# Matmul and layer norm on one core: the row-tile transposes move from TensorE to VectorE, and the start and the end of the kernel are rewritten

## The chip, the cores and the metric

The kernel runs on one core of a Trainium2 chip. The metric is device time in microseconds (us), the median over several executions. The profile of one execution has a span, from its first to its last instruction, which is about 2 us shorter than the timed value. In the profile PE is TensorE (PEld its weight loads), DVE is VectorE, ACT is ScalarE, POOL is GpSimd and SP is SyncE. L107 means line 107 of that kernel's file.

A ratio quoted below is the mean time of one kernel's fast runs over that of the fast runs of the kernel before in the same rounds, so it is not quite the ratio of the medians.

## The reference

```python
def setup_inputs():            # m = k = n = 2048, all float32
    return {"a": (2048, 2048), "b": (2048, 2048), "gamma": (2048,), "beta": (2048,), "eps": 1e-5}   # shapes, shortened

def reference(a, b, gamma, beta, eps):
    x = np.matmul(a, b)
    mean = np.mean(x, axis=-1, keepdims=True)
    var = np.var(x, axis=-1, keepdims=True)
    return gamma * (x - mean) / np.sqrt(var + eps) + beta
```

## The kernel before

The product is cut into 16 row tiles of 128 rows and 4 quarters of 512 columns. One (tile, quarter) needs 16 matmuls, one for each contraction tile of 128, and fills one PSUM tile of 128x512 fp32, called a bank here: 1024 matmuls in all. The program holds eight banks: seven for the product and one for transposes in this kernel, eight for both in the changed one. Each matmul needs the piece of `a` transposed. Both inputs are cast to fp16 while they are loaded.

Transposing is done on TensorE, for every tile, eight pieces into the one transpose bank, which ACT then copies out:

```python
    def emit_transposes_half(i, h):
        a16 = a16_lst[i]
        at = at_lst[i]
        t_ps = psum.tile([P, n_kt // 2, P], FP16, tag="tps", bufs=1, ...)
        for j in range(n_kt // 2):
            nc.tensor.transpose(t_ps[:, j, :], a16[:, ts(h * 8 + j, P)], ident)
        nc.scalar.copy(at[:, ds(h * 8, 8), :], t_ps)
```

The start takes the first four row tiles together with the left half of `b` (two quarters), so that each row of `b` that lands feeds eight matmuls. The loads bring tile 0, a row of `b`, tile 1, and so on, then the rest of `b`:

```python
    a16_lst[0] = emit_a_load(0, split=4)
    nc.gpsimd.dma_start(b16[:, 0, 0:NH], b[ts(0, P), 0:NH])
    ...
    a16_lst[1] = emit_a_load(1, split=2)
    nc.gpsimd.dma_start(b16[:, 1, 0:NH], b[ts(1, P), 0:NH])
    ...
    for kt in range(3, n_kt):
        nc.gpsimd.dma_start(b16[:, kt, 0:NH], b[ts(kt, P), 0:NH])
```

The scheduler of the framework chooses the order of instructions on each engine. In the steady part a tile's matmuls run over contraction tiles outside and quarters inside; the transposes of tile i+2 stand among them. Then each quarter gets its statistics (DVE) and is copied to SBUF (ACT), and DVE normalises from the copy with two operations per quarter:

```python
            for kt in range(n_kt):
                for q in range(n_nb):
                    emit_mm(i, q, kt)
                if kt == 4 and i + 2 < n_mt:
                    alloc_at(i + 2)
                    emit_transposes_half(i + 2, 0)
                if kt == 9 and i + 2 < n_mt:
                    emit_transposes_half(i + 2, 1)
            for q in range(n_nb):
                quarter_done(i, q)          # bn_stats on DVE, copy to SBUF on ACT
        emit_ln_stats(i)
        ...
        emit_ln_stt(i, ...)                 # 2 scalar_tensor_tensor per quarter on DVE, then the output DMA
```

Of the kernel before, what the change touches and what calls it, by code (L numbers as in the profile page):

```python
# [9 lines left out]
FP32 = mybir.dt.float32  # L10
FP16 = mybir.dt.float16
AluOp = mybir.AluOpType
# [4 lines left out]
def kernel(  # L17
# [9 lines left out]
    nc = tc.nc  # L27
    P = 128
    M, K = a.shape
    K2, N = b.shape  # L30
    assert K == K2
    assert M % P == 0 and K % P == 0 and N % 2048 == 0
    n_mt = M // P
    n_kt = K // P
    NB = 512
    n_nb = N // NB
    NH = N // 2

    n_start = 4
    assert n_mt > n_start  # L40

    if isinstance(eps, bass.AP):
        eps_ap = eps
        eps_val = None
    else:
        eps_ap = None
        eps_val = float(eps)

    konst = ctx.enter_context(tc.tile_pool(name="konst", bufs=1))
    bpool = ctx.enter_context(tc.tile_pool(name="bpool", bufs=1))  # L50
    a16p = ctx.enter_context(tc.tile_pool(name="a16p", bufs=4))
    atp = ctx.enter_context(tc.tile_pool(name="atp", bufs=6))
    xpool = ctx.enter_context(tc.tile_pool(name="xpool", bufs=20))
    upool = ctx.enter_context(tc.tile_pool(name="upool", bufs=4))
    cpool = ctx.enter_context(tc.tile_pool(name="cpool", bufs=2))
    stat = ctx.enter_context(tc.tile_pool(name="stat", bufs=4))
    psum = ctx.enter_context(tc.tile_pool(name="psum", bufs=1, space=bass.MemoryType.PSUM))

    gamma_b = konst.tile([P, N], FP32)
    beta_b = konst.tile([P, N], FP32)  # L60
    eps_t = konst.tile([P, 1], FP32)
    ident = konst.tile([P, P], FP16)

    b16 = bpool.tile([P, n_kt, N], FP16)

    def emit_a_load(i, split=1):
        a16 = a16p.tile([P, K], FP16, tag="a16", name=f"a16_{i}")
        w = K // split
        for s in range(split):
            nc.gpsimd.dma_start(a16[:, ds(s * w, w)], a[ts(i, P), ds(s * w, w)])  # L70
        return a16

    a16_lst = [None] * (n_mt + 2)
    at_lst = [None] * (n_mt + 1)

    def alloc_at(i):
        at_lst[i] = atp.tile([P, n_kt, P], FP16, tag="at", name=f"at{i}")

    def emit_transposes_half(i, h):
        a16 = a16_lst[i]  # L80
        at = at_lst[i]
        t_ps = psum.tile([P, n_kt // 2, P], FP16, tag="tps", bufs=1,
                         name=f"tps{i}_{h}")
        for j in range(n_kt // 2):
            nc.tensor.transpose(t_ps[:, j, :], a16[:, ts(h * 8 + j, P)], ident)  # L85
        nc.scalar.copy(at[:, ds(h * 8, 8), :], t_ps)  # L86

    def emit_transposes(i):
        alloc_at(i)
        emit_transposes_half(i, 0)  # L90
        emit_transposes_half(i, 1)
        return at_lst[i]

    bnst_l = [None] * n_mt
    c_ps_l = [[None] * n_nb for _ in range(n_mt)]
    x_sb_l = [[None] * n_nb for _ in range(n_mt)]
    rstd_l = [None] * n_mt
    mv_l = [None] * n_mt

    def alloc_q(i, q):  # L100
        if bnst_l[i] is None:
            bnst_l[i] = stat.tile([P, n_nb, 6], FP32, tag="bnst", name=f"bnst{i}")
        c_ps_l[i][q] = psum.tile([P, NB], FP32, tag="c_ps", bufs=7,
                                 name=f"cps_{i}_{q}")

    def emit_mm(i, q, kt):
        nc.tensor.matmul(  # L107
            c_ps_l[i][q],
            at_lst[i][:, kt, :],
            b16[:, kt, ds(q * NB, NB)],  # L110
            start=(kt == 0),
            stop=(kt == n_kt - 1),
        )

    def quarter_done(i, q):
        nc.vector.bn_stats(bnst_l[i][:, q, :], c_ps_l[i][q])  # L116
        x_sb = xpool.tile([P, NB], FP32, tag="x_sb", name=f"x_{i}_{q}")
        nc.scalar.copy(x_sb, c_ps_l[i][q])  # L118
        x_sb_l[i][q] = x_sb

    def emit_ln_stats(i):
        mv = stat.tile([P, 2], FP32, name=f"mv{i}")
        nc.vector.bn_aggr(mv, bnst_l[i])  # L123
        ve = stat.tile([P, 1], FP32, name=f"ve{i}")
        nc.vector.tensor_tensor(ve, mv[:, 1:2], eps_t, AluOp.add)  # L125
        sq = stat.tile([P, 1], FP32, name=f"sq{i}")
        nc.scalar.activation(sq, ve, ActFn.Sqrt)  # L127
        rstd = stat.tile([P, 1], FP32, name=f"rstd{i}")
        nc.vector.reciprocal(rstd, sq)  # L129
        mv_l[i] = mv  # L130
        rstd_l[i] = rstd

    def emit_ln_stt(i, split_out=2):
        mv, rstd = mv_l[i], rstd_l[i]
        c_sb = cpool.tile([P, N], FP32, tag="c_sb", name=f"c{i}")
        nq_per_out = n_nb // split_out
        for q in range(n_nb):
            qs = ds(q * NB, NB)
            u = upool.tile([P, NB], FP32, tag="u", name=f"u_{i}_{q}")
            nc.vector.scalar_tensor_tensor(  # L140
                u, x_sb_l[i][q], mv[:, 0:1], gamma_b[:, qs],
                AluOp.subtract, AluOp.mult,
            )
            nc.vector.scalar_tensor_tensor(  # L144
                c_sb[:, qs], u, rstd, beta_b[:, qs],
                AluOp.mult, AluOp.add,
            )
            if (q + 1) % nq_per_out == 0:
                o = ds((q + 1 - nq_per_out) * NB, nq_per_out * NB)
                nc.sync.dma_start(out[ts(i, P), o], c_sb[:, o])  # L150

    a16_lst[0] = emit_a_load(0, split=4)
    nc.gpsimd.dma_start(b16[:, 0, 0:NH], b[ts(0, P), 0:NH])
    nc.vector.memset(ident, 0.0)
    nc.gpsimd.affine_select(
        out=ident, in_=ident, compare_op=AluOp.not_equal, fill=1.0,
        base=0, pattern=[[-1, P]], channel_multiplier=1,
    )
    if eps_ap is not None:
        nc.sync.dma_start(eps_t, eps_ap.unsqueeze(0).to_broadcast([P, 1]))  # L160
    else:
        nc.vector.memset(eps_t, eps_val)
    a16_lst[1] = emit_a_load(1, split=2)
    nc.gpsimd.dma_start(b16[:, 1, 0:NH], b[ts(1, P), 0:NH])  # L164
    a16_lst[2] = emit_a_load(2, split=2)
    nc.gpsimd.dma_start(b16[:, 2, 0:NH], b[ts(2, P), 0:NH])  # L166
    a16_lst[3] = emit_a_load(3, split=2)
    for kt in range(3, n_kt):
        nc.gpsimd.dma_start(b16[:, kt, 0:NH], b[ts(kt, P), 0:NH])  # L169
    a16_lst[4] = emit_a_load(4)  # L170
    a16_lst[5] = emit_a_load(5)
    for kt in range(n_kt):
        nc.gpsimd.dma_start(b16[:, kt, NH:N], b[ts(kt, P), NH:N])  # L173
    nc.gpsimd.dma_start(gamma_b, gamma.unsqueeze(0).to_broadcast([P, N]))  # L174
    nc.gpsimd.dma_start(beta_b, beta.unsqueeze(0).to_broadcast([P, N]))  # L175
    for i in range(6, n_mt):
        a16_lst[i] = emit_a_load(i)

    startup_pairs_L = [(p, q) for p in range(n_start) for q in (0, 1)]
    startup_pairs_R = [(p, q) for p in range(n_start) for q in (2, 3)]  # L180
    for (p, q) in startup_pairs_L:
        alloc_q(p, q)
    for i in range(n_start):
        alloc_at(i)
    emit_transposes_half(0, 0)
    emit_transposes_half(0, 1)
    for q in (0, 1):
        emit_mm(0, q, 0)
    for p in range(1, n_start):
        emit_transposes_half(p, 0)  # L190
        emit_transposes_half(p, 1)
        for pp in range(p):
            for q in (0, 1):
                emit_mm(pp, q, p)
        for kt in range(p + 1):
            for q in (0, 1):
                emit_mm(p, q, kt)
    for kt in range(n_start, n_kt):
        for (p, q) in startup_pairs_L:
            emit_mm(p, q, kt)  # L200
    for (p, q) in startup_pairs_L:
        quarter_done(p, q)
    for (p, q) in startup_pairs_R:
        alloc_q(p, q)
    for kt in range(n_kt):
        for (p, q) in startup_pairs_R:
            emit_mm(p, q, kt)
        if kt == 0:
            at_lst[4] = emit_transposes(4)
        if kt == 2:  # L210
            at_lst[5] = emit_transposes(5)
    for (p, q) in startup_pairs_R:
        quarter_done(p, q)
    for p in range(n_start):
        emit_ln_stats(p)

    for i in range(n_start, n_mt):
        last = i == n_mt - 1
        for q in range(n_nb):
            alloc_q(i, q)  # L220
        if last:
            for q in range(n_nb):
                for kt in range(n_kt):
                    emit_mm(i, q, kt)
                quarter_done(i, q)
        else:
            for kt in range(n_kt):
                for q in range(n_nb):
                    emit_mm(i, q, kt)
                if kt == 4 and i + 2 < n_mt:  # L230
                    alloc_at(i + 2)
                    emit_transposes_half(i + 2, 0)
                if kt == 9 and i + 2 < n_mt:
                    emit_transposes_half(i + 2, 1)
            for q in range(n_nb):
                quarter_done(i, q)
        emit_ln_stats(i)
        if i - n_start < n_start:
            emit_ln_stt(i - n_start)
        emit_ln_stt(i, split_out=(2 if not last else 4))  # L240


# [32 lines left out]
```

## Time and profile before

| | |
|---|---|
| time | 268.0 us median of 15 (267.13 to 268.71) |
| span of the profiled execution | 265.8 us |
| TensorE busy | 242.6 us, of which product matmuls 230.0 |
| start of the last statistics (TensorE is done) | 255.16 us |
| DVE / ACT busy | 131.9 / 74.1 us |

Lines of the page of the kernel before: busy time by engine, then the chain of work that ended last (shares of the span), then groups of instructions (line, engine, operation, output from input, shapes, count, then busy us, mean ns of one, and idle time before with what ended it).

```profile
PE 242.6 (91%) x1280; PEld 116.6 (44%) x1280; DVE 131.9 (50%) x242; ACT 74.1 (28%) x114; POOL 30.2 (11%) x61
...
PE 89%; DMA 6%; DVE 2%; issue 1%; POOL 0%; DVEq 0%; POOLq 0%
PE cps L107 84%; PE tps L85 5%; DMA b<-in_b_dram 4%; DMA a<-in_a_dram 2%; DVE u L140 1%; DVE c L144 1%; POOL a L70 0%; DVE bnst L116 0%; DVEq L270 0%; DVE mv L123 0%; DVE ve L125 0%; DVE rstd L129 0%; POOLq L256 0%
...
L107 PE MATMUL cps<-b,at 128*128 128x512 f16 x1024 | 230.0, 381 | 5.6 <-DMA b<-in_b_dram 5.6
...
L85 PE MATMUL tps<-ident,a 128*128 128x128 f16 x256 | 22.3, 231 | 6.9 <-DMA a<-in_a_dram 6.8
```

The chain is 89% PE: whatever is taken from TensorE in the steady part comes off the time, as long as TensorE stays the chain there. The mean of 381 ns of one matmul overlaps with its neighbours (they are 0.2167 us apart, as the next lines show), so it is no cost. The cost is read from the chain in order of time (start us, length us, what), here the end of the start and then a stretch of the steady part:

```profile
8.22 9.45 DMA b<-in_b_dram
17.67 0.04 issue
17.71 1.01 PE cps L107 x2
18.72 0.85 PE tps L85 x8
19.57 2.13 PE cps L107 x5
...
88.62 0.45 PE tps L85 x8
89.07 9.55 PE cps L107 x44
98.62 0.45 PE tps L85 x8
99.07 4.32 PE cps L107 x20
103.38 0.45 PE tps L85 x8
```

In the steady part 64 matmuls take 9.55 + 4.32 = 13.87 us, 0.2167 us each, and 16 transposes take 0.90 us, 0.056 us each.

### The profile page before, as it was taken

How to read it: one execution, taken by the hardware profiler on the slowest of the kernel's cores; microseconds unless marked ns; L12 is line 12 of the kernel's file. 1: busy time of each engine (PE TensorE's matmuls, PEld its weight loads, DVE VectorE, ACT ScalarE, POOL GpSimd, SP SyncE). 2: the span in 40 equal slices, each digit the busy share in tenths (PEclk: the TensorE clock that was granted, in tenths of full speed). 3: DMA queues.
4: the chain of work that ended last, by engine and by line, in shares of the span. 5: the costliest groups of instructions: out<-in, count | busy, mean ns of one | idle time of the engine just before them, and what ended most of it. 6: DMA issues, size and time to landing. Idle time of an engine off the chain costs nothing.

```text
span 265.8 us, 3149 instructions
## 1 busy us (share of the span) xinstructions
PE 242.6 (91%) x1280; PEld 116.6 (44%) x1280; DVE 131.9 (50%) x242; ACT 74.1 (28%) x114; POOL 30.2 (11%) x61
## 2 busy tenths in 40 slices
PE   1369999999999999999999999999999999999930
PEld 1135444454444444454444444454544444444410
DVE  0000002400079089898989092745739091837753
ACT  1325101640064142323224151333133151303110
POOL 8443333440000000000000000000000000000000
PEclk9999999999999999999999999999999999999985
DMA  5999999999931615939375605230302112030304
GB/s 69 183 210 209 210 214 208 208 213 368 215 69 72 146 22 167 226 161 196 152 154 211 156 13 181 50 158 0 147 13 80 79 47 113 0 158 2 158 0 158
DMA packets 12974, 35.85 MB, mean 135 GB/s; under 512 B 1440, under 2 KB 1952, under 8 KB 12704
## 3 DMA queue, kind: packets, MB, share of 16 engines
q0 software_dynamic: 8064, 18.88, 37.7%
q1 hardware_dynamic: 4896, 16.78, 15.8%
q8 instruction: 10, 0.16, 0.3%
q14 instruction: 4, 0.03, 0.0%
HBM read 35.65 MB, written 16.78 MB: 197 GB/s over the span
## 4 chain that ended last, share of the span: by engine, by line
PE 89%; DMA 6%; DVE 2%; issue 1%; POOL 0%; DVEq 0%; POOLq 0%
PE cps L107 84%; PE tps L85 5%; DMA b<-in_b_dram 4%; DMA a<-in_a_dram 2%; DVE u L140 1%; DVE c L144 1%; POOL a L70 0%; DVE bnst L116 0%; DVEq L270 0%; DVE mv L123 0%; DVE ve L125 0%; DVE rstd L129 0%; POOLq L256 0%
## 5 line engine op out<-in xcount | busy, mean ns | idle before, releaser
L107 PE MATMUL cps<-b,at 128*128 128x512 f16 x1024 | 230.0, 381 | 5.6 <-DMA b<-in_b_dram 5.6
L107 PEld LDWEIGHTS <-at 128*128 128x128 f16 x1024 | 99.4, 98 | 121.0 <-issue 9.6
L116 DVE BATCH_NORM_STATS2 bnst<-cps 128x6 f32<-128x512 f32 x64 | 40.0, 685 | 127.8 <-PE cps L107 127.8
L118 ACT COPY x<-cps 128x512 f32<-128x512 f32 x64 | 37.3, 585 | 100.0 <-DVE bnst L116 99.1
L86 ACT COPY at<-tps 128x1024 f16<-128x1024 f16 x32 | 32.4, 1012 | 81.3 <-PE tps L85 81.3
L140 DVE SCALAR_TENSOR_TENSOR u<-x,mv,gamma_b 128x512 f32<-128x512 f32 x64 | 45.9, 743 | 0.0
L144 DVE SCALAR_TENSOR_TENSOR c<-u,rstd,beta_b 128x512 f32<-128x512 f32 x64 | 45.1, 745 | 0.0
L85 PE MATMUL tps<-ident,a 128*128 128x128 f16 x256 | 22.3, 231 | 6.9 <-DMA a<-in_a_dram 6.8
L85 PEld LDWEIGHTS <-a 128*128 128x128 f16 x256 | 18.6, 104 | 17.1 <-DMA a<-in_a_dram 7.6
L70 POOL DMA_DIRECT2D a<-in_a_dram x22 | 11.9, 548 | 106.1 <-PE tps L85 99.6
L173 POOL DMA_DIRECT2D b<-in_b_dram x16 | 8.4, 527 | 14.9 <-DMA b<-in_b_dram 11.0
L169 POOL DMA_DIRECT2D b<-in_b_dram x13 | 6.9, 527 | 9.7 <-DMA b<-in_b_dram 5.1
L123 DVE BATCH_NORM_AGGREGATE mv<-bnst 128x2 f32<-128x24 f32 x16 | 3.9, 254 | 0.4
L127 ACT ACTIVATE sq<-ve 128x1 f32<-128x1 f32 x16 | 3.1, 203 | 0.6 <-DVE ve L125 0.6
L125 DVE TENSOR_TENSOR ve<-mv,eps_t 128x1 f32<-128x1 f32 x16 | 2.3, 155 | 0.4
L129 DVE RECIPROCAL rstd<-sq 128x1 f32<-128x1 f32 x16 | 2.4, 157 | 0.3 <-ACT sq L127 0.3
L86 ACT ACT_TABLE_LOAD x1 | 1.3, 1283 | 0.7 <-PEq L256 0.7
L127 ACT ACT_TABLE_LOAD x1 | 1.3, 1283 | 0.0
L166 POOL DMA_DIRECT2D b<-in_b_dram x1 | 0.5, 532 | 1.2 <-DMA a<-in_a_dram 1.2
L175 POOL DMA_DIRECT2D beta_b<-in_beta_dram x1 | 0.5, 527 | 0.7 <-DMA b<-in_b_dram 0.7
L174 POOL DMA_DIRECT2D gamma_b<-in_gamma_dram x1 | 0.5, 527 | 0.7 <-DMA b<-in_b_dram 0.7
L164 POOL DMA_DIRECT2D b<-in_b_dram x1 | 0.6, 585 | 0.0
(8 smaller groups left out, 1.5 us busy)
## 6 DMA issues: line engine op xcount, KB each, us to landing
out_dram<-c SPq DMA_DIRECT2D x30, 512.0 KB, 2.6
b<-in_b_dram POOLq DMA_DIRECT2D x32, 256.0 KB, 9.7
a<-in_a_dram POOLq DMA_DIRECT2D x12, 512.0 KB, 9.6
a<-in_a_dram POOLq DMA_DIRECT2D x6, 256.0 KB, 9.7
gamma_b<-in_gamma_dram POOLq DMA_DIRECT2D x1, 1024.0 KB, 11.0
beta_b<-in_beta_dram POOLq DMA_DIRECT2D x1, 1024.0 KB, 12.2
out_dram<-c SPq DMA_DIRECT2D x4, 256.0 KB, 2.6
a<-in_a_dram POOLq DMA_DIRECT2D x4, 128.0 KB, 4.8
```

What stands on the lines that cost most here:

```text
L70: nc.gpsimd.dma_start(a16[:, ds(s * w, w)], a[ts(i, P), ds(s * w, w)])
L85: nc.tensor.transpose(t_ps[:, j, :], a16[:, ts(h * 8 + j, P)], ident)
L86: nc.scalar.copy(at[:, ds(h * 8, 8), :], t_ps)
L107: nc.tensor.matmul(c_ps_l[i][q], at_lst[i][:, kt, :], b16[:, kt, ds(q * NB, NB)], start=(kt == 0), stop=(kt == n_kt - 1),)
L116: nc.vector.bn_stats(bnst_l[i][:, q, :], c_ps_l[i][q])
L118: nc.scalar.copy(x_sb, c_ps_l[i][q])
L123: nc.vector.bn_aggr(mv, bnst_l[i])
L127: nc.scalar.activation(sq, ve, ActFn.Sqrt)
L140: nc.vector.scalar_tensor_tensor(u, x_sb_l[i][q], mv[:, 0:1], gamma_b[:, qs], AluOp.subtract, AluOp.mult,)
L144: nc.vector.scalar_tensor_tensor(c_sb[:, qs], u, rstd, beta_b[:, qs], AluOp.mult, AluOp.add,)
L169: nc.gpsimd.dma_start(b16[:, kt, 0:NH], b[ts(kt, P), 0:NH])
L173: nc.gpsimd.dma_start(b16[:, kt, NH:N], b[ts(kt, P), NH:N])
```

## The change

The intent: take the transposes of tiles 4 to 15 off TensorE; begin the first matmuls in step with the loads; give TensorE zero matmuls while it waits, in the hope of a full clock; spare ACT's copies; shorten the end. The diff, cut to its core:

```diff
+    b_rows = b.rearrange("(c p t) n -> c t p n", p=P, t=4)
+    a_pieces = a.rearrange("(s r) (c q k) -> q c r s k", r=32, c=4, q=4)
 # loads of tiles 4.. come as pairs of tiles, in 16 pieces that place 32-row blocks
+    def load_pair(i):
+        pair = a16p.tile([P, 8, 4, P], FP16, tag="a16", name=f"a{i}")
+        for c in range(4):
+            for q in range(4):
+                nc.gpsimd.dma_start(
+                    pair[ds(32 * q, 32), :, c], a_pieces[q, c][:, ds(4 * i, 8)])
+        a_in[i], a_in[i + 1] = pair[:, 0:4], pair[:, 4:8]
-            nc.tensor.transpose(t_ps[:, j, :], a16[:, ts(h * 8 + j, P)], ident)
-        nc.scalar.copy(at[:, ds(h * 8, 8), :], t_ps)
+    def transpose_part(i, c):
+        nc.vector.transpose(
+            at[i][:, ds(4 * c, 4), :].rearrange("p t (j r) -> p j t r", r=32),
+            a_in[i][:, :, c].rearrange("p j (k t) -> p j t k", t=4),
+        )
 # the order on all engines is that of the program text
+    with tc.manual_schedule(engines=order):
+        for _ in range(9):
+            nc.tensor.matmul(w_ps, warm[:, 0:P], warm, start=True, stop=True)      # zeros
 # start: loads in chunks of four contraction tiles
+        for c in range(4):
+            for g in range(G):
+                if g or c:
+                    load_first(g, c)              # 128 rows x 512 columns of a
+                load_b(4 * c + g, 0, NH)
 ...
 # start: chunk 0 in step with its loads; chunk c then while chunk c+1 is transposed; chunk 3 bank by bank
+            if c in (1, 2):
+                for t in kts:
+                    for g, q in early:            # 7 of the 8 banks; the eighth holds transposes
+                        mm(g, q, t)
+                    transpose_first(t % 4, c + 1)
+        for g, q in early:
+            for t in range(12, n_kt):
+                mm(g, q, t)
+            stats(g, q)
+            evacuate(g, q)
 # steady part: quarter outside, contraction tile inside; no copy, DVE normalises from PSUM one tile later
+            if i > G:
+                normalise(i - 1)
+            for q in range(n_nb):
+                bank(i, q)
+                for t in range(n_kt):
+                    mm(i, q, t)
+                stats(i, q)
+                if i + 2 < n_mt:
+                    transpose_part(i + 2, q)
+                if q == 3 and i < 3 * G:
+                    normalise((i - G) // 2, (i - G) % 2)     # half of one of tiles 0 to 3
 # end: the last quarter of the last tile on ACT and POOL, the others on DVE
+        nc.scalar.activation(y, x_of[i, 3], ActFn.Identity, bias=shift, scale=rs_of[i])
+        nc.gpsimd.tensor_tensor(y, y, gamma_b[:, q3], AluOp.mult)
+        nc.gpsimd.tensor_tensor(c[:, q3], y, beta_b[:, q3], AluOp.add)
```

The load already puts each column block of `a` on its group of 32 partitions, and the DVE transpose then has to exchange rows and columns within each 32x32 block. Within a chunk of 512 contraction indices, partition p and step t stand for index 4p + t, in `a` and in `b` alike; the sum does not depend on that order, and the runs in memory become 512 bytes long instead of 128.

## The prediction

> **What bounds the kernel now.** TensorE. The page gives PE 242.6 us busy of a 265.8 us span; the chain that ended last is 89% PE (84% product matmuls, 5.3% transposes into tps, about 14 us). The chain in order of time shows the product matmuls back to back at 0.2165 us (152 in 32.93 us), so 1024 need 221.7 us. The rest of the span is the start, the transposes and the tail:
> - Start: the windows show PE nearly idle until 17.7 us, waiting for loads (5.6 us on b, 6.8 us on a). 112 matmuls and the first 64 transposes are done at 45.8 us. [...] 208 to 214 GB/s as written in fp16.
> - Transposes of row tiles 4 to 15: 192, in groups of 8 taking 0.45 us, about 11 us, all on the chain.
> - Tail: last matmul ends at 255.16 us, last DVE operation at 261.7, span at 265.8: 10.6 us.
>
> DVE (131.9 us) and ACT (74.1 us) are not limits.
>
> **What the change does.**
> 1. TensorE loses those 192 transposes: -11 us, directly on the chain. DVE gets 48 transposes of 128x512 instead. [...] a 512-element DVE operation here takes 0.65 us start to start, so I estimate 0.7 us each, 34 us in all.
> 2. The start loads a and b in chunks of four contraction tiles. The left half of b and four row tiles (6 MB in fp16) must land: from the bandwidth of before, at about 34 us. Only 28 matmuls (6.1 us) then remain: 112 matmuls done at about 40.3 us instead of 45.8: -5.5 us. The zero matmuls fill waits and cost nothing on the chain.
> 3. Later tiles are normalised straight from PSUM: ACT copies fall from 64 to 16. A PE stall is not expected: banks have over 10 us of slack.
> 4. Tail: three of four quarters end on DVE, the fourth on ACT and POOL; about -1.3 us.
>
> **New risks on the chain.** DVE per steady tile: 4 statistics (2.5), 8 scalar_tensor_tensor (5.4), 4 transposes (2.8), small ones (0.4): 11.1 us, under PE's 13.9 us; with half an old tile (tiles 4 to 11) 14 us or slightly more. DVE falls a few us behind and recovers after tile 12, with PE unaffected. The loads of a become 16 pieces per pair, 512 B read and 256 B written per descriptor. [...] An issue took 0.53 us, so a pair needs at least 8.5 us; I expect the first pair to land at 62 to 67 us, while PE wants tile 4 at about 71 us. I allow 1.5 us for stalls there and at the bank handover.
>
> **Sum.** 43.8 (128 matmuls done) + 194 (896 x 0.2165) + 1.5 + 9.3 (tail) = 248.6 us span; launch times are 2 us above the span: **250.5 us**, 8 in 10 within 246 to 257. Faster by over 2%: 0.95; within 2%: 0.04; slower: 0.01.
>
> **What would show each step.** PE chain: no transposes after about 33 us, product matmuls still 0.2165 us; 112 matmuls done near 40 us; DVE busy 165 to 175 us, transposes 0.6 to 0.8 us each; ACT busy near 25 us; last matmul near 239 us, 9 to 10 us before the end.
>
> **What would make it wrong.** Small descriptors so slow that DVE waits for pairs (waits of DVE transposes on loads of a) and PE stalls at tiles 4 to 6; strided b rows (four rows apart) lowering start bandwidth below 200 GB/s; DVE transposes well above 1 us, which would make DVE the limit.

The 208 to 214 GB/s are the rates of slices 3 to 9 on the page of the kernel before. The 1.5 us for stalls are an allowance and the over 10 us of slack an estimate of mine.

## More of the kernel before

(Clock records are the stretches for which a trace tells the granted TensorE clock; outside them the reader of the profile prints 1.)

A marker of the start that every variant of this kernel has is the statistics of the eighth PSUM bank: it begins when the first 128 matmuls are done. From the timeline of DVE before (start us, length us, engine, line, operation, count, and in brackets the idle time before and what ended it):

```profile
49.59 0.70 DVE L116 BATCH_NORM_STATS2 bnst<-cps 128x6 f32<-128x512 f32 x1 [0.73 <-PE cps L107]
```

## The result

The changed kernel takes 251.97 us (median of 9, 250.9 to 252.31) against 268.0 us; the ratio is 0.9395, 95% interval 0.938 to 0.941. It is 16.0 us faster. The results are correct.

The same parts of the page of the changed kernel:

```profile
PE 236.6 (95%) x1121; PEld 106.8 (43%) x1121; DVE 162.9 (65%) x282; ACT 22.1 (9%) x43; POOL 84.4 (34%) x153
...
PE 81%; DMA 13%; DVE 2%; POOL 2%; issue 1%; POOLq 0%
...
L99 PE MATMUL ps<-b,at 128*128 128x512 f16 x1024 | 223.4, 379 | 0.4 <-DMA b<-in_b_dram 0.3
...
L90 DVE STREAM_TRANSPOSE at<-a 128x512 f16<-128x512 f16 x48 | 32.8, 690 | 15.8 <-DMA a<-in_a_dram 15.8
```

PE busy fell by only 6.0 us although 192 transposes left it, mostly because 33 zero matmuls came in (4.0, 3.5 and 3.2 us busy by the page); busy time is thus no measure of the gain here. The chain in order of time is:

```profile
21.33 8.70 DMA b<-in_b_dram
30.04 0.28 issue
30.32 7.33 DMA b<-in_b_dram
37.65 0.04 issue
37.69 202.47 PE ps L99 x937
240.16 0.02 issue
240.18 0.71 DVE bnst L107
```

After 37.69 us TensorE does product matmuls and nothing else, without a break, up to 240.16 us. Until then the chain is the loads. The 937 are the last 25 of the first 112 matmuls, the 16 of the eighth bank and the 896 of the middle part. In the first bank the three matmuls that need rows 12 to 14 of `b` ran before row 15 landed, so 25 and not 28 were left at 37.69 us. Timeline of PE:

```profile
36.72 0.81 PE L99 MATMUL ps<-b,at 128*128 128x512 f16 x3
```

The marker of the eighth bank, from the timeline of DVE of the changed kernel:

```profile
46.74 0.70 DVE L107 BATCH_NORM_STATS2 bnst<-ps 128x6 f32<-128x512 f32 x1 [2.75 <-PE ps L99]
```

With the marker, the 15.8 us between the two spans split into three parts:

| part | before | after | difference |
|---|---|---|---|
| start, to the eighth bank's statistics | 49.59 | 46.74 | -2.85 |
| from there to the last bank's statistics | 205.57 | 193.44 | -12.13 |
| from there to the end of the span | 10.64 | 9.82 | -0.82 |

The middle part holds the same 896 matmuls in both. After the change they take 193.44 / 896 = 0.2159 us each. Eight of the variants below (b, b2, the three of c, d, e and j), which have no transposes on TensorE in this part either, take the same 193.44 us. So the steady part stands at one pace in all nine; whether TensorE could go faster is not shown. As long as it needs these 896 matmuls at that pace, what is left to gain lies in the start and the end.

### The profile page after: what moved, and what is told of

The parts are those of the page before. It is cut to its first block, busy times and chain, and to the rows that moved or that the text cites. A ratio compares the mean times of both kernels' runs of the same rounds, so it can differ in the third digit from the quotient of the medians.

```text
span 250.0 us, 2909 instructions
## 1 busy us (share of the span) xinstructions
PE 236.6 (95%) x1121; PEld 106.8 (43%) x1121; DVE 162.9 (65%) x282; ACT 22.1 (9%) x43; POOL 84.4 (34%) x153
## 4 chain that ended last, share of the span: by engine, by line
PE 81%; DMA 13%; DVE 2%; POOL 2%; issue 1%; POOLq 0%
PE ps L99 81%; DMA b<-in_b_dram 13%; POOL f L66 1%; DVE c L134 1%; DVE ps L128 1%; POOL b L62 1%; DVE bnst L107 0%; POOL ident L190 0%; DVE mv L116 0%; POOLq L190 0%; DVE rs L124 0%; DVE shift L162 0%; POOLq L295 0%
## 5 line engine op out<-in xcount | busy, mean ns | idle before, releaser
L99 PE MATMUL ps<-b,at 128*128 128x512 f16 x1024 | 223.4, 379 | 0.4 <-DMA b<-in_b_dram 0.3
L82 POOL DMA_DIRECT2D a<-in_a_dram x96 | 54.8, 581 | 65.5 <-DVE at L90 50.9
L107 DVE BATCH_NORM_STATS2 bnst<-ps 128x6 f32<-128x512 f32 x64 | 43.2, 684 | 32.3 <-PE ps L99 32.3
L90 DVE STREAM_TRANSPOSE at<-a 128x512 f16<-128x512 f16 x48 | 32.8, 690 | 15.8 <-DMA a<-in_a_dram 15.8
L134 DVE SCALAR_TENSOR_TENSOR c<-u,rs,beta_b 128x512 f32<-128x512 f32 x60 | 42.2, 744 | 0.0
L128 DVE SCALAR_TENSOR_TENSOR u<-ps,mv,gamma_b 128x512 f32<-128x512 f32 x44 | 31.6, 742 | 0.4
L111 ACT COPY x<-ps 128x512 f32<-128x512 f32 x16 | 9.4, 585 | 30.8 <-DVE bnst L107 30.8
L128 DVE SCALAR_TENSOR_TENSOR u<-x,mv,gamma_b 128x512 f32<-128x512 f32 x16 | 11.4, 734 | 0.6 <-ACT sq L118 0.5
L66 POOL DMA_DIRECT2D f<-in_a_dram x16 | 8.8, 551 | 5.0 <-PE t_ps L72 2.1
L226 PE MATMUL ps<-warm 128*128 128x512 f16 x12 | 3.5, 402 | 0.0
L220 PE MATMUL ps<-warm 128*128 128x512 f16 x12 | 3.2, 379 | 0.0
```

The costliest lines, as they stand in the source:

```text
L66: nc.gpsimd.dma_start(f.rearrange("m p t -> m (p t)"), a[ts(g, P), ts(c, 4 * P)])
L82: nc.gpsimd.dma_start(pair[ds(32 * q, 32), :, c], a_pieces[q, c][:, ds(4 * i, 8)])
L90: nc.vector.transpose(at[i][:, ds(4 * c, 4), :].rearrange("p t (j r) -> p j t r", r=32), a_in[i][:, :, c].rearrange("p j (k t) -> p j t k" ...
L99: nc.tensor.matmul(x_of[i, q], at[i][:, kt, :], b16[:, kt, ds(q * NB, NB)], start=(kt == 0), stop=(kt == n_kt - 1),)
L107: nc.vector.bn_stats(bnst[i][:, q, :], x_of[i, q])
L111: nc.scalar.copy(x, x_of[i, q])
```

## The experiments

Twelve runs of eleven variants were made, all correct. The changed kernel was not run again beside them, so a variant is compared with it through the ratios, whose intervals are 0.5 to 1.4 us to each side, and through the traces. "Marker" is the start of the eighth bank's statistics and "last" that of the last bank's, both from the profiled execution.

| run | marker | last | span | median us | ratio | 95% |
|---|---|---|---|---|---|---|
| before | 49.59 | 255.16 | 265.8 | 268.0 | 1 | |
| changed | 46.74 | 240.18 | 250.0 | 251.97 | 0.9395 | 0.938 to 0.941 |
| a_pe_transposes | 46.09 | 250.25 | 261.7 | 264.38 | 0.9865 | 0.9825 to 0.9905 |
| b_no_zeros | 48.88 | 242.32 | 252.1 | 252.56 | 0.9425 | 0.9372 to 0.9478 |
| b2_no_zeros | 47.09 | 240.53 | 250.3 | 252.34 | 0.9397 | 0.9376 to 0.9418 |
| c_triangle | 44.18 | 237.62 | 247.5 | 249.47 | 0.9314 | 0.9272 to 0.9357 |
| c2_triangle | 44.12 | 237.56 | 247.4 | 249.46 | 0.9306 | 0.9285 to 0.9327 |
| c3_triangle | 45.50 | 238.94 | 248.7 | 250.38 | 0.9324 | 0.9304 to 0.9345 |
| d_kt_outer | 46.49 | 239.93 | 249.7 | 251.36 | 0.938 | 0.9346 to 0.9413 |
| e_start_before | 46.61 | 240.05 | 249.9 | 252.06 | 0.9406 | 0.9385 to 0.9428 |
| f_tail_dve | slow | slow | slow | 252.3 | 0.9419 | 0.9395 to 0.9444 |
| h_before_zeros | 52.59 | 258.17 | 268.8 | 269.45 | 1.0056 | 1.0029 to 1.0083 |
| i_before_manual | 47.98 | 258.21 | 268.8 | 271.36 | 1.01 | 1.0078 to 1.0122 |
| j_evacuate | 46.81 | 240.25 | 250.1 | 251.67 | 0.938 | 0.9353 to 0.9407 |

### a_pe_transposes: the transposes back on TensorE

```diff
-        for c in range(4):
-            for q in range(4):
-                nc.gpsimd.dma_start(pair[ds(32 * q, 32), :, c], a_pieces[q, c][:, ds(4 * i, 8)])
+        for j in (i, i + 1):
+            row = a16p.tile([P, 4, P, 4], FP16, tag="a16", name=f"a{j}", bufs=4)
+            nc.gpsimd.dma_start(row.rearrange("m c p t -> m (c p t)"), a[ts(j, P), :])
 ...
-        nc.vector.transpose(...)
+        t_ps = psum.tile([P, 4, P], FP16, tag="c_ps", bufs=8, name=f"t_ps{i}_{c}")
+        for t in range(4):
+            nc.tensor.transpose(t_ps[:, t, :], a_in[i][:, c, :, t], ident)
+        nc.scalar.copy(at[i][:, ds(4 * c, 4), :], t_ps)
```

The transposes of tiles 4 and 5 also had to move behind the first banks that come free, because at their old place all eight banks are taken.

> Undoes one part of the changed kernel: row tiles 4 to 15 are loaded as whole rows and transposed on TensorE again (192 transposes, copied out of PSUM by ACT). My theory (most of the gain is TensorE time, the transposes stood on its chain): about 10 to 11 us slower than the changed kernel, so 262 to 263 us; DVE busy falls by about 33 us and that changes nothing. Rival (the gain is from the new start, the clock or DVE reading PSUM, and the transposes hid in waits): within 2 us of the changed kernel, 251 to 254 us.

Measured: 264.38 us, 12.4 us slower than the changed kernel. The chain in order of time shows a group of transposes after every 16 matmuls as a step between their starts (the short lines of the transposes themselves were left out of this answer, which lists the longest pieces):

```profile
207.88 3.45 PE ps L97 x16
211.56 3.45 PE ps L97 x16
215.24 3.45 PE ps L97 x16
```

The starts are 3.68 us apart and 16 matmuls take 3.45, so four transposes take 0.23 us of TensorE. From the marker to the last statistics this kernel needs 204.16 us against 193.44: 10.72 us for 192 transposes, 56 ns each. The rival, that they hide in waits, is out. Of the 12.4 us, 10.1 are there when TensorE ends (250.25 against 240.18). A further 1.6 us of the profiled execution lie between the last DVE operation and the end of the span (255.89 to 261.7, against 245.81 to 250.0), where only output transfers are left. Why these took longer was not followed up.

### e_start_before: the old start in the changed kernel

```diff
-        for c in range(4):
-            for g in range(G):
+        for g in range(G):
+            for c in range(4):
                 if g or c:
                     load_first(g, c)
-                load_b(4 * c + g, 0, NH)
+            if g < 3:
+                load_b(g, 0, NH)
+        for t in range(3, n_kt):
+            load_b(t, 0, NH)
 # and on TensorE: all transposes of tile g, then the matmuls of rows 0 to g of b that it allows; 24 of the 33 zeros are gone
```

> The changed kernel with the start of the kernel before: row tiles 0 to 3 loaded whole with the first rows of b between them, then the rest of the left half of b; TensorE in the matching order; zero matmuls kept in part; all else as changed. My theory (the new start is worth the 2.1 us that the traces show between 45.8 and 43.7 us for 112 matmuls): 1.5 to 3 us slower than the changed kernel, 253.5 to 255 us. Rival (both starts end one chunk after the same last load, so the order is worth nothing): within 0.7 us.

Measured: 252.06 us, ratio 0.9406 against 0.9395 for the changed kernel. The marker is at the same place:

```profile
46.61 0.70 DVE L107 BATCH_NORM_STATS2 bnst<-ps 128x6 f32<-128x512 f32 x1 [2.75 <-PE ps L99]
```

So the new order of loads, with the order of matmuls that goes with it, is worth nothing by itself, and my theory fell. The two starts reach 46.7 us by different roads: in this one the chain is TensorE from 14.38 us on, at half clock until 19.51 us by the clock record; in the changed kernel the chain is the loads until 37.65 us and 25 matmuls then remain. By the landing records of the traces the last row of the left half of `b` is there at 37.28 us in this kernel, at 37.65 us in the changed one and at 37.58 us in the kernel before. So the loads of the start end together in all three, and the later marker of the kernel before comes from TensorE.

### i_before_manual: the kernel before, with TensorE in the order of its program text

```diff
+    with tc.manual_schedule(engines={mybir.EngineType.PE}):
         ...                                    # the body as it was
+    late_L, late_R = startup_pairs_L.pop(), startup_pairs_R.pop()     # eighth bank of each half: after the other seven
```

> The kernel before with its TensorE instructions in the order of its own program text, instead of the order that the scheduler chose; the last of eight banks of each half is done after the other seven, as the seven banks demand; loads and all else as before. In the scheduler's order transposes of row tiles 1 and 2 stand behind matmuls that wait for rows 1 and 2 of b. My theory (that order, not the order of loads, costs the kernel before 2 us against the changed kernel's start): 1.5 to 2.5 us faster than the kernel before, 265.5 to 266.5 us. Rival (the start ends when the loads and a low clock allow, whatever the order): within 0.6 us.

Measured: 271.36 us, 1.0% slower than before. The theory was half right, and the total went the other way. The marker moved as expected, by 1.6 us:

```profile
47.98 0.70 DVE L116 BATCH_NORM_STATS2 bnst<-cps 128x6 f32<-128x512 f32 x1 [0.74 <-PE cps L107]
```

But the text order makes TensorE wait where the scheduler's order did not: for the one bank of transposes, which ACT has to empty (four waits in the first 24 us, two of 1.10 us after the marker), and in every tile for one of seven banks. From the waits, from the chain between 104 and 113 us, and from the timeline of PE:

```profile
PE tps L85 <- ACT at L86: 6.6, 6, 1.1
```

```profile
104.93 4.55 PE cps L107 x21
...
109.50 0.71 DVE bnst L116
...
110.29 0.59 ACT x L118
...
110.92 1.24 PE cps L107 x5
```

```profile
110.92 3.83 PE L107 MATMUL cps<-b,at 128*128 128x512 f16 x17 [0.17 <-ACT x L118]
```

The first line reads: 6.6 us in 6 waits, the longest 1.1 us. The second fence has 1.4 us of statistics and copy on the chain between two runs of matmuls; TensorE works on other banks meanwhile and stands idle for 0.17 us only. A tile then takes 15.03 us (104.93 to 119.96) instead of about 14.8. From the marker to the last statistics this kernel needs 210.23 us against 205.57. The run shows that 1.6 us of the 2.85 us at the start can be had by changing TensorE's order alone. Why is not shown, for the clock moved with the order: the first record of the full clock begins at 21.95 us in the kernel before, at 17.16 us in this one and at 6.21 us in the changed kernel. In the kernel before the chain is TensorE from 17.71 us on, so 4.24 us of it were at half pace (0.43 us per matmul), which costs about 2.1 us (an estimate, half of 4.24). That is a rival for most of the 2.85 us, and no run separates it from the order. The two profiled executions of the kernel without zeros below point the same way: with the full clock from 17.21 us on (and a relapse) the marker stands at 48.88 us, with the full clock from 12.08 us on at 47.09. The change also uses four-piece transposes with copies on two engines, and these were not tried alone.

### h_before_zeros: zero matmuls in the waits of the kernel before

```diff
+    def zeros(p, n):
+        for _ in range(n):
+            nc.tensor.matmul(c_ps_l[p][0], warm[:, 0:P], warm, start=True, stop=True)
+    zeros(0, 18)
     ...
+    zeros(0, 3)
     ...
+        if p < 3:
+            zeros(p, 9)
```

> The kernel before with zero matmuls added into its waits of the first 17 us, nothing else. Its trace has matmuls 0.43 us apart between 17.7 and 21.7 us. My theory (that is a low clock after a wait, and costs it about 1 to 1.5 us against a start that keeps TensorE working): 0.7 to 1.5 us faster than the kernel before. Rival (the start is bound by the loads all the same): within 0.4 us.

Measured: 269.45 us, 0.6% slower. The marker is 3.0 us later than before: one group of nine zeros lies on the chain after the loads had come (2.79 us at 21.88), and the row of `b` that TensorE waits for landed at 19.10 us instead of 17.67, for a reason that was not followed up. The clock record is full from 6.41 us but falls to half from 20.06 to 23.47 us, so the zeros did not keep it up either. This run does not isolate what the low clock costs; it shows that these zeros were not free once the data were there.

### b_no_zeros and b2_no_zeros: the changed kernel without the zeros

```diff
-        for _ in range(9):
-            nc.tensor.matmul(w_ps, warm[:, 0:P], warm, start=True, stop=True)
+        nc.tensor.matmul(w_ps, warm[:, 0:P], warm, start=True, stop=True)
 # and the groups of three in chunks 0 and 1 are gone
```

> The changed kernel without 32 of its 33 zero matmuls. My theory (they only fill waits of a start that is bound by the loads, and the kernel before had a full clock without them): 251 to 252.5 us, within 0.5 us of the changed kernel. Rival (they keep the TensorE clock up): matmuls of the first 40 us at 0.43 us apart for some stretches, and 2 to 6 us slower than the changed kernel.

> The kernel without 32 zero matmuls once more, with more rounds, as its first run spread over 3 us. If the zeros are worth what its trace shows (matmuls 0.43 us apart from 9 to 17 us, TensorE done 2.2 us later): 1 to 2.5 us slower than the changed kernel, 253 to 254.5 us. If nothing: 251.7 to 252.3 us.

Measured: 252.56 us (251.18 to 254.2, 4 runs), then 252.34 us (251.8 to 252.85, 5 runs). In the second the ratio equals the changed kernel's. The two profiled executions of this same kernel differ. Timeline of PE, first execution, then the second:

```profile
9.32 2.74 PE L99 MATMUL ps<-b,at 128*128 128x512 f16 x6 [0.52 <-DVE at L74]
11.86 0.63 PE L72 MATMUL t_ps<-ident,f 128*128 128x128 f16 x4
13.17 4.31 PE L99 MATMUL ps<-b,at 128*128 128x512 f16 x10 [0.68 <-ACT at L76]
...
23.63 2.79 PE L99 MATMUL ps<-b,at 128*128 128x512 f16 x7
```

```profile
9.43 2.74 PE L99 MATMUL ps<-b,at 128*128 128x512 f16 x6 [0.52 <-DVE at L74]
11.97 0.45 PE L72 MATMUL t_ps<-ident,f 128*128 128x128 f16 x4
13.09 2.33 PE L99 MATMUL ps<-b,at 128*128 128x512 f16 x10 [0.68 <-ACT at L76]
```

Ten matmuls take 4.31 us in one execution and 2.33 us in the other. In the first, the slow stretches pushed the marker to 48.88 us; in the second, the loads bound the start and it came at 47.09. So without zeros the clock was low for some of the start, for a time that varied between the two executions: the full clock is recorded from 17.21 us on in the first, with half clock again from 24.04 to 27.45, and from 12.08 us on in the second, against 6.21 us with the zeros. The 1.00 that the reader prints for 13 to 17 us of the first, before its first record, is no measurement: the ten matmuls from 13.17 us on are 0.43 us apart. Where there is a record (half clock from 24.04 us on) the spacing agrees with it: 7 matmuls in 2.79 us from 23.63 us on. In the second execution this hides behind the loads. One of the nine executions without zeros took 254.2 us and the other eight at most 252.85, against 252.31 at most with them; whether the zeros take away such late executions, so few do not show. My sentence that the kernel before had a full clock without them was wrong, as its 5 matmuls in 2.13 us show.

### c_triangle, c2_triangle, c3_triangle: matmuls as soon as their data are there

In the changed kernel TensorE does a chunk's matmuls while the next chunk is transposed, so after the last load nearly a whole chunk, 25 matmuls, remains. These kernels keep the loads and change the order on TensorE; the 12 zeros of chunk 1 fall away:

```diff
+        def ready(g, c):     # matmuls that tile g's chunk c and b row 4c+g make possible
+            for t in range(4 * c, 4 * c + g + 1):
+                for gg, q in early:
+                    if gg <= g and (gg == g or t == 4 * c + g):
+                        yield gg, q, t
 # c_triangle, chunks 1 to 3: transpose piece (g, c), then the matmuls made ready by the piece before
+                transpose_first(g, c)
+                for m in held:
+                    mm(*m)
+                held = list(ready(g, c))
 # after the last piece: what is held except row 15, then row 15, bank by bank
```

`c2_triangle` puts half of the held matmuls ahead of the transposes and drops 9 zeros of chunk 0. `c3_triangle` goes back to transposes first, keeps three matmuls over for the next step, and drops the same zeros.

> The changed kernel with one change of order in the start: in every chunk, not only the first, TensorE does a matmul as soon as its row of b and its piece of a are there, so that after the last row of b only 7 matmuls remain of the first 112 instead of 28. My theory (the start ends one chunk of TensorE work, 6 us, after the last load, because TensorE works one chunk behind the loads): the 112 matmuls end 3 to 4.5 us earlier, 247.5 to 249 us. Rival (TensorE itself is full in the start, so order can't help): within 1 us of the changed kernel, 251 to 252.5 us.

> The version with matmuls as soon as their data are there, with two more changes: half of the matmuls that are possible go ahead of the wait for the next piece of a, and of the 12 zero matmuls of the first chunk 9 are left out. My theory (after the last load TensorE still had 17 matmuls to do besides the last 7, now none or few): 1 to 1.5 us faster than the first version of that order, 248 to 248.7 us. Rival (the clock drops without the zeros): slower than the first version, with a granted clock under 1 in the first 30 us.

> The second version of matmuls as soon as their data are there, with three matmuls held back to stand between the transposes of one piece and those of the next, so that TensorE doesn't wait for the copy of a transposed piece. In the second version's trace TensorE is busy or waits for such copies from 10.4 us on. My theory (the start is now bound by TensorE and these waits, 0.5 to 0.8 us each): 0.5 to 1.5 us faster, 248 to 249 us. Rival (the last load bounds it again): within 0.3 us of 249.5 us.

Measured: ratios 0.9314, 0.9306 and 0.9324. The first version gains 2.6 us at the marker, a little less than the 3 to 4.5 us expected (its 249.47 us, too, lie just above 247.5 to 249), and keeps it to the end (237.62 against 240.18). Timeline of DVE in c_triangle:

```profile
39.43 4.28 DVE L107 BATCH_NORM_STATS2 bnst<-ps 128x6 f32<-128x512 f32 x7 [2.60 <-PE ps L99]
44.18 0.70 DVE L107 BATCH_NORM_STATS2 bnst<-ps 128x6 f32<-128x512 f32 x1 [0.46 <-PE ps L99]
```

The rival, that TensorE is full and order can't help, is out. The two refinements brought nothing, and their theories fell: in c2_triangle the chain is TensorE and its waits for copies from 10.42 us on (with the full clock recorded from 4.82 us, so the rival of a low clock is out as well), in c3_triangle it goes back to waits for pieces of `a` (7.09 us, ending at 36.6). Loads and TensorE are now about equally long, and relieving one meets the other. c_triangle and c2_triangle, at about 249.5 us, beat both kernels.

### d_kt_outer: the order of the steady matmuls

```diff
-            for q in range(n_nb):
-                bank(i, q)
+            if not last:
+                for q in range(n_nb):
+                    bank(i, q)
                 for t in range(n_kt):
-                    mm(i, q, t)
+                    for q in range(n_nb):
+                        mm(i, q, t)
 ...                                            # the last tile as it was
```

> The changed kernel with the matmul order of the kernel before in tiles 4 to 14: contraction tile outside, quarter inside, so that consecutive matmuls go to four banks in turn. In the traces the steady matmuls of the kernel before are 0.2167 us apart and those of the changed kernel 0.2155. If the order makes that: 0.6 to 0.9 us slower than the changed kernel. Rival (the transposes in between, or ACT and DVE reading PSUM, make it): no difference beyond 0.3 us.

Measured: 251.36 us, ratio 0.938: no difference. From marker to last statistics it takes 193.44 us, the same as the changed kernel. So the order over banks does not explain why the kernel before takes 205.57 us for this part and a_pe_transposes, with the same number of transposes, 204.16. The 1.4 us in between stay open. i_before_manual shows that waits for seven banks and one transpose bank can cost that much, but it is another order.

### j_evacuate: ACT copies back in the steady part

```diff
                 stats(i, q)
+                if not last:
+                    evacuate(i, q)
```

> The changed kernel with part 3 undone: ACT copies each quarter of tiles 4 to 14 out of PSUM after its statistics, as in the kernel before, and DVE normalises from the copy in SBUF. My theory (ACT has room, banks have over 10 us of slack, DVE takes 0.742 us from PSUM against 0.734 us from SBUF, so nothing on the chain changes): within 0.5 us of the changed kernel, 251.5 to 252.5 us. Rival (reading PSUM directly gave part of the gain): 1 us or more slower.

Measured: 251.67 us, ratio 0.938, and the last statistics at 240.25 us: no difference. Sparing ACT 44 copies and letting DVE read PSUM changed nothing in the time. It gave DVE neither a gain nor a loss: scalar_tensor_tensor on 128x512 took 0.742 us with one of its two inputs in PSUM, 0.734 us with both in SBUF (means on the page of the changed kernel).

### f_tail_dve: the whole last tile on DVE

```diff
-        nc.scalar.activation(y, x_of[i, 3], ActFn.Identity, bias=shift, scale=rs_of[i])
-        nc.gpsimd.tensor_tensor(y, y, gamma_b[:, q3], AluOp.mult)
-        nc.gpsimd.tensor_tensor(c[:, q3], y, beta_b[:, q3], AluOp.add)
-        for q in range(3):
+        for q in range(n_nb):
 ...                                            # and the output of the fourth quarter from SP
```

> The changed kernel with the whole last tile normalised on DVE, as in the kernel before, instead of one quarter on ACT and POOL. My theory (the DVE chain after the last statistics is two operations longer, minus the shift, so 1.2 us): 1.0 to 1.3 us slower than the changed kernel. Rival (the end is set by the output transfers, which are the same): within 0.4 us.

Measured: 252.3 us, ratio 0.9419: 0.3 us over the changed kernel by the medians, which would fit the rival, and 0.6 us by the ratios, which is between both theories; the intervals overlap. The split of the last tile is worth less than I expected, perhaps nothing; this is inconclusive.

One of its five executions took 652.88 us, and it was the profiled one. Its chain and its line of cores:

```profile
80.45 559.69 PE ps L99 x940
640.16 0.71 DVE bnst L107
```

```profile
core 0: 650.9 us, clock 1.000
```

940 matmuls in 559.69 us are 0.595 us each, 2.8 times the usual, from beginning to end, while DVE's statistics took their usual time. The 1.000 is no measurement: this trace holds no clock record at all, and the reader of the profile prints 1 where there is none. What slowed TensorE is not known. It was the only such execution, and the four others of this kernel took 252.23 to 253.41 us, so it says nothing about the edit.

## Why the prediction was right, and where it was off

The measured 251.97 us lie within the range, and 1.5 us over the point value. The main mechanism was right and its size too: 11 us of transposes predicted, 10.7 us measured by putting them back. Of the 15.8 us between the spans these 10.7 are shown; the 2.85 us of the start are measured but not traced to one cause, 1.4 us of the middle part stay open, and the 0.8 us of the end are not settled, as f_tail_dve is inconclusive. That the total came within 1.5 us is partly luck, for the sum hides errors of opposite sign:

| term | predicted | measured | off by |
|---|---|---|---|
| "128 matmuls done" | 43.8 | 46.74 | +2.9 |
| 896 matmuls and stalls | 194 + 1.5 | 193.44 | -2.1 |
| tail | 9.3 | 9.82 | +0.5 |
| span | 248.6 | 250.0 | +1.4 |
| timed minus span | 2 | 1.97 | 0 |

- **Step 2 of the prediction, "The left half of b and four row tiles (6 MB in fp16) must land ... at about 34 us", is the mis-sized term.** The last row landed at 37.65 us. The amount was rounded down, for one: four tiles are 2.10 MB and half of b 4.19 MB, 6.29 MB together, 1.4 us more at 206 GB/s (an estimate). Most of the rest is that I took the time by which as many bytes had moved for the time at which the last of them had landed: up to 37.7 us the windows add up to 6.73 MB, so 0.44 MB of later loads had moved as well, 2.1 us at 206 GB/s (an estimate). The bandwidth was a little under the 208 to 214 GB/s foreseen, 203 to 206 between 13.6 and 37.7 us. The gain of the start was therefore 2.85 us at the marker, where 5.5 was foreseen for the 112 matmuls. e_start_before shows that the order of the loads, to which step 2 ascribed it, gives none of it; i_before_manual shows that TensorE's order can give 1.6 us.
- "Only 28 matmuls (6.1 us) then remain" was nearly right: 25 remained, 0.65 us less, which took back a little of the late landing. c_triangle shows that they need not remain.
- "The zero matmuls fill waits and cost nothing on the chain" was right (b2_no_zeros).
- "A PE stall is not expected" from reading PSUM was right, and j_evacuate confirms that this part is worth nothing. The slack was a little smaller than foreseen: by DVE's timeline the first bank of tile 4 is read out at 93.94 us, and tile 6 needs it at 74.3 + 128 x 0.2159 = 101.9 us (an estimate from the marker), 8 us later.
- The allowance of 1.5 us for stalls was not needed. The loads of pairs do delay DVE, but not TensorE. Waits and DVE's timeline after the change:

```profile
DVE at L90 <- DMA a<-in_a_dram: 15.8, 4, 11.9
```

```profile
65.39 3.08 DVE L90 STREAM_TRANSPOSE at<-a 128x512 f16<-128x512 f16 x5 [1.67 <-DMA a<-in_a_dram]
68.39 3.65 DVE L107 BATCH_NORM_STATS2 bnst<-ps 128x6 f32<-128x512 f32 x6
```

  DVE waits 15.8 us for pairs, nearly all of it before tile 4 begins. The transposes of tiles 4 and 5 end at about 68.5 us. TensorE wants tile 4 at 46.7 + 128 x 0.2159 = 74.3 us (an estimate from the marker), so some 6 us were to spare.
- DVE transposes take 0.69 us on average (0.669 to 0.714), where 0.7 was estimated; DVE is 162.9 us busy, just under the 165 to 175 foreseen. Between 100 and 200 us it is busy for 19.0 to 19.7 of every 20 us, so it has little room left, but it does not stop TensorE. ACT is 22.1 us busy, where near 25 was foreseen.
- What the 512-byte runs of the pairs' loads cost, this case does not decide: between 58.0 and 63.3 us, with pieces of a pair under way, the windows give 102 GB/s against 198 to 211 just before, but POOL was busy issuing for 5.13 of these 5.3 us, so short runs and issue time are not told apart. POOL needed 0.581 us on average to issue one of the 96 pieces of 64 KB, and 0.533 us for one of 256 KB, so 16 pieces take about 9.3 us (an estimate from the 0.581 us), although each has a quarter of the bytes.

## What to carry to other kernels

Where TensorE was on the chain without a break, the price of each of its instructions could be read from the chain (here 56 ns for a transpose, 216 ns for a matmul). Moving 192 transposes to an engine with room gained just that, 10.7 us, and moving copies off ACT, which is not on the chain, gained nothing (251.67 us with them back, 251.97 without). At a start that is bound by loads, ask what is still to be done when the last byte has landed: an order that does each piece as it lands gained 2.6 us here, while another order of loads, zero matmuls and freed copies gained nothing measurable (0.9406, 0.9397 and 0.938 when undone, 0.9395 with them). Before a new order is credited with a gain in the start, look in the clock records from when on the full clock is granted (21.95, 17.16 and 6.21 us in three kernels here). Undo the parts of a large rewrite one at a time, and use a marker in the timeline that all variants share.
